# A mixture-of-experts kernel on one core: hand-set semaphores and a looped TensorE program in place of a scheduled, unrolled one

## The chip, the core and the metric

The kernel runs on one core of a Trainium2 chip. A core has a matrix engine (TensorE, "PE" in the profile, with its weight loads listed apart as "PEld"), a vector engine (VectorE, DVE), a scalar engine (ScalarE, ACT), GpSimd (POOL) and SyncE (SP), and 16 transfer engines that move data between the large memory (HBM) and the on-chip memory (SBUF). TensorE writes its sums to PSUM, from where VectorE and ScalarE copy them out. Engines run on their own and wait for one another by semaphores.

The metric is the device time of one execution in microseconds (us), the median of several runs.

## The reference

Eight experts, each with its own 256 tokens: a matrix product, a ReLU, a second matrix product. Inputs and output are fp32.

```python
n_experts, capacity, hidden, expert_hidden = 8, 256, 512, 2048
# x [8, 256, 512], w1 [8, 512, 2048], w2 [8, 2048, 512]
h = np.matmul(x, w1)
h = np.maximum(h, 0)
return np.matmul(h, w2).astype(np.float32)
```

x is 4.19 MB, w1 and w2 are 33.55 MB each, the output is 4.19 MB.

## The kernel before

The weights are cast from fp32 to bf16 on their way into SBUF, by transfers that GpSimd issues. Expert weights are loaded in pairs; each of w1 and w2 has two buffers of two experts. Only the last pair is loaded one expert at a time, and w2 of expert 7 in two halves. In w1 each partition holds four rows of an expert (32 KB read in one piece), in w2 sixteen rows (32 KB too).

```python
w1_v = w1.rearrange("e (p ko) n -> p e (ko n)", ko=K1)      # K1 = 4, P = 128
w2_v = w2.rearrange("e (p j) n -> p e (j n)", p=P)          # j = 16
...
GROUPS = [(0, 1), (2, 3), (4, 5), (6, 7)]
W1_LOADS = [(g,) for g in GROUPS[:-1]] + [((6,),), ((7,),)]
W2_LOADS = [(g, 0, K2) for g in GROUPS[:-1]] + [((6,), 0, K2), ((7,), 0, 8), ((7,), 8, K2)]
...
def load_w1(es):
    ...
    nc.gpsimd.dma_start(w1t[g][:, i:i + len(es), :], w1_v[:, es[0]:es[-1] + 1, :])
```

x comes in two transfers (1 MB through SyncE, then cast by VectorE; the rest through GpSimd) and is transposed on TensorE, 64 blocks of 128x128. Layer 1 of an expert is 64 matmuls of 256 columns, with w1 as the stationary operand; ScalarE applies the ReLU while it moves two blocks of F (128x512) at a time from PSUM to hT. Layer 2 is 32 matmuls of 512 columns, with hT as the stationary operand.

```python
def layer1(e):
    ...
    for pr in range(K2 // 2):
        h_ps = psum_h.tile([P, 2, C], FP32, name="h_ps")
        for s in range(2):
            j = pr * 2 + s
            for ko in range(K1):
                nc.tensor.matmul(h_ps[:, s, :], w1_r[:, ko, :, j], xT[:, ko, :, e, :],
                                 start=(ko == 0), stop=(ko == K1 - 1))
        nc.scalar.activation(hT[:, pr * 2:pr * 2 + 2, :]..., h_ps[:]..., Relu)
    return hT

def layer2(e, hT):
    ...
    for k, m in order:
        nc.tensor.matmul(o_ps[m][:], hT[:, k, m * P:(m + 1) * P],
                         w2t[g][:, e - g[0], k * H:(k + 1) * H],
                         start=(k == 0), stop=(k == K2 - 1))
        if k == K2 - 1:
            ...   # VectorE (for the last expert also ScalarE) copies o_ps to out_sb or out_last
```

For the first three pairs both first layers run before both second layers. The output of experts 0 to 6 leaves in one transfer of 3.67 MB; ahead of it, and before the last half of w2, stands a store of 3 KB to the same place, which the large one has to wait for. The output of expert 7 leaves by itself, through SyncE.

```python
for e, hT in zip(g, hs):
    layer2(e, hT or layer1(e))
    if e == 5:
        issue(E, E)
        store_first()
        loads.append(tail)      # the last half of w2 of expert 7
        issue(E, E)
    if e == E - 2:
        store()
nc.sync.dma_start(out_v[:, E - 1, :], out_last[:].rearrange("p m h -> p (m h)"))
```

Everything is unrolled: each matmul is an instruction of its own in TensorE's program, and the framework places the semaphores.

Of the kernel before, what the change touches and what calls it, by code (L numbers as in the profile page):

```python
# [1 line left out]

# [5 lines left out]

FP32 = mybir.dt.float32  # L10
BF16 = mybir.dt.bfloat16


@with_exitstack
def kernel(
    ctx: ExitStack,
    tc: tile.TileContext,
    x: bass.AP,
    w1: bass.AP,
    w2: bass.AP,  # L20
    out: bass.AP,
):
    nc = tc.nc
    P = 128
    E, C, H = x.shape
    F = w1.shape[2]
    MC = C // P
    K1 = H // P
    K2 = F // P

    R = E * C // P

    x_v = x.rearrange("e (pp r) k -> (e pp) (r k)", r=R)
    w1_v = w1.rearrange("e (p ko) n -> p e (ko n)", ko=K1)
    w2_v = w2.rearrange("e (p j) n -> p e (j n)", p=P)
    out_v = out.rearrange("e (p mo) k -> p e (mo k)", mo=MC)

    GROUPS = [(0, 1), (2, 3), (4, 5), (6, 7)]
    W1_LOADS = [(g,) for g in GROUPS[:-1]] + [((6,),), ((7,),)]
    W2_LOADS = [(g, 0, K2) for g in GROUPS[:-1]] + [((6,), 0, K2), ((7,), 0, 8), ((7,), 8, K2)]
    NG = max(len(g) for g in GROUPS)
    GROUP = {e: g for g in GROUPS for e in g}

    const = ctx.enter_context(tc.tile_pool(name="const", bufs=1))
    w1_pool = ctx.enter_context(tc.tile_pool(name="w1_pool", bufs=4 // NG))  # L50
    w2_pool = ctx.enter_context(tc.tile_pool(name="w2_pool", bufs=4 // NG))
    hT_pool = ctx.enter_context(tc.tile_pool(name="hT_pool", bufs=2))
    psum_t = ctx.enter_context(tc.tile_pool(name="psum_t", bufs=2, space=bass.MemoryType.PSUM))
    psum_h = ctx.enter_context(tc.tile_pool(name="psum_h", bufs=3, space=bass.MemoryType.PSUM))
    psum_o = ctx.enter_context(tc.tile_pool(name="psum_o", bufs=3, space=bass.MemoryType.PSUM))

    identity = const.tile([P, P], BF16, name="identity")
    xT = const.tile([P, K1, MC, E, P], BF16, name="xT")
    out_sb = const.tile([P, E - 1, MC, H], FP32, name="out_sb")
    out_last = const.tile([P, MC, H], FP32, name="out_last")  # L60

    HEAD = 4
    x_head = const.tile([P, HEAD * H], FP32, name="x_head")
    x_sb = w2_pool.tile([P, NG, K2 * H], BF16, name="w2_sb")[:, 0, :]

    w1t, w2t = {}, {}

    def load_x():
        nc.gpsimd.dma_start(x_sb[:, HEAD * H:], x_v[:, HEAD * H:])  # L69

    def load_w1(es):
        g = GROUP[es[0]]
        if es[0] == g[0]:
            w1t[g] = w1_pool.tile([P, NG, K1 * F], BF16, name="w1_sb")
        i = es[0] - g[0]
        nc.gpsimd.dma_start(w1t[g][:, i:i + len(es), :], w1_v[:, es[0]:es[-1] + 1, :])  # L76

    def load_w2(es, a, b):
        g = GROUP[es[0]]
        if es[0] == g[0] and a == 0:  # L80
            w2t[g] = w2_pool.tile([P, NG, K2 * H], BF16, name="w2_sb")
        i = es[0] - g[0]
        nc.gpsimd.dma_start(  # L83
            w2t[g][:, i:i + len(es), a * H:b * H],
            w2_v[:, es[0]:es[-1] + 1, a * H:b * H],
        )

    def store_first():


        nc.gpsimd.dma_start(  # L91
            out_v[:16, 0:5:2, :16], out_sb[:16, 0:5:2, 0, :16]
        )

    def store():
        nc.gpsimd.dma_start(  # L96
            out_v[:, :E - 1, :], out_sb[:].rearrange("p e m h -> p e (m h)")
        )

    def transpose_x():  # L100


        x_r = x_sb.rearrange("p (r2 m q ko) -> p r2 m q ko", m=MC, q=P, ko=K1)
        for i, (ko, m) in enumerate((ko, m) for ko in range(K1) for m in range(MC)):
            ps = psum_t.tile([P, R // MC, P], BF16, name="xt_ps")
            for r2 in range(R // MC):
                nc.tensor.transpose(ps[:, r2, :], x_r[:, r2, m, :, ko], identity[:])  # L107
            src = ps[:].rearrange("k r2 ep -> k ep r2")
            dst = xT[:, ko, m].rearrange("k e (pp r2) -> k (e pp) r2", r2=R // MC)
            if i % 2:  # L110
                nc.scalar.copy(dst, src)  # L111
            else:
                nc.vector.tensor_copy(dst, src)  # L113

    def layer1(e):
        g = GROUP[e]
        w1_r = w1t[g][:, e - g[0], :].rearrange("p (ko q j) -> p ko q j", ko=K1, j=K2)
        hT = hT_pool.tile([P, K2, C], BF16, name="hT")
        for pr in range(K2 // 2):
            h_ps = psum_h.tile([P, 2, C], FP32, name="h_ps")  # L120
            for s in range(2):
                j = pr * 2 + s
                for ko in range(K1):
                    nc.tensor.matmul(  # L124
                        h_ps[:, s, :],
                        w1_r[:, ko, :, j],
                        xT[:, ko, :, e, :],
                        start=(ko == 0),
                        stop=(ko == K1 - 1),
                    )  # L130
            nc.scalar.activation(  # L131
                hT[:, pr * 2:pr * 2 + 2, :].rearrange("p a c -> p (a c)"),
                h_ps[:].rearrange("p a c -> p (a c)"),
                mybir.ActivationFunctionType.Relu,
            )
        return hT

    def layer2(e, hT):
        g = GROUP[e]
        last = e == E - 1  # L140
        o_ps = [psum_o.tile([P, H], FP32, name="o_ps") for _ in range(MC)]
        if last:
            order = [(k, m) for k in range(K2) for m in range(MC)]
        else:
            order = [(k, m) for m in range(MC) for k in range(K2)]
        for k, m in order:
            nc.tensor.matmul(  # L147
                o_ps[m][:],
                hT[:, k, m * P:(m + 1) * P],
                w2t[g][:, e - g[0], k * H:(k + 1) * H],  # L150
                start=(k == 0),
                stop=(k == K2 - 1),
            )
            if k == K2 - 1:
                if last and m == 1:
                    nc.scalar.copy(out_last[:, m, :], o_ps[m][:])  # L156
                elif last:
                    nc.vector.tensor_copy(out_last[:, m, :], o_ps[m][:])  # L158
                else:
                    nc.vector.tensor_copy(out_sb[:, e, m, :], o_ps[m][:])  # L160

    loads = []
    for i, g in enumerate(GROUPS):
        own = [(load_w1, l) for l in W1_LOADS if l[0][0] in g]
        own += [(load_w2, l) for l in W2_LOADS if l[0][0] in g]
        own.sort(key=lambda f: (f[1][0][0], f[0] is load_w2))
        loads += [(i, *f) for f in own]
    tail = loads.pop()  # L170

    def issue(ready1, ready2):

        while loads:
            i, f, l = loads[0]
            if i >= (ready1 if f is load_w1 else ready2):
                break
            loads.pop(0)
            f(*l)

    B = 4 // NG
    nc.sync.dma_start(x_head[:], x_v[:, :HEAD * H])
    nc.vector.tensor_copy(x_sb[:, :HEAD * H], x_head[:])  # L183
    with tc.manual_schedule(engines={mybir.EngineType.PE, mybir.EngineType.Pool}):
        load_x()
        make_identity(nc, identity)
        issue(B, B - 1)
        transpose_x()
        for i, g in enumerate(GROUPS):
            issue(i + B, i + B)  # L190
            whole = len(g) > 1 and (g,) in W1_LOADS
            if whole:
                hs = [layer1(e) for e in g]
                issue(i + 1 + B, i + B)
            else:
                hs = [None] * len(g)
            for e, hT in zip(g, hs):
                layer2(e, hT or layer1(e))
                if e == 5:
                    issue(E, E)  # L200
                    store_first()
                    loads.append(tail)
                    issue(E, E)
                if e == E - 2:
                    store()
    nc.sync.dma_start(out_v[:, E - 1, :], out_last[:].rearrange("p m h -> p (m h)"))

# [1 line left out]
_INS = ['x', 'w1', 'w2']  # L209
# [26 lines left out]
```

## Time and profile before

| what | value |
|---|---|
| time, median of 3 runs | 181.25 us (181.23 to 181.43) |
| span of the profiled execution | 179.7 us |
| layer 1 matmuls, mean of 512 | 285 ns |
| layer 2 matmuls, mean of 248 | 393 ns |
| ReLU evictions, mean of 64 | 597 ns |
| copies of o_ps by VectorE, mean of 14 | 692 ns |
| loads of a pair of experts (6), issue to landing, median | 62.1 us |
| loads of one expert (3), issue to landing, median | 51.5 us |

The span is the profiled execution from its first to its last instruction; the time of a run is a little longer than it. A matmul's duration is that of one record from start to end: matmuls overlap, so that 64 of layer 1 take 7.15 us together. "Issue to landing" counts the time that a transfer stands behind others in the queue. In the slices, a digit is the busy share in tenths of one fortieth of the span.

### The profile page before, as it was taken

The numbers are of one execution on the slowest core, as the hardware profiler recorded it, in microseconds if no ns is written. First come the engines' busy times: TensorE is split into PE (matmuls) and PEld (weight loads), VectorE is DVE, ScalarE is ACT, GpSimd is POOL, SyncE is SP. The second block draws the span as 40 slices with busy tenths as digits, with TensorE's granted clock in tenths as the row PEclk, the third lists the DMA queues.
The fourth block names the chain that finished last, engine by engine and source line by source line (L and its number), as shares of the span: only waits on it lengthen the run. The fifth ranks groups of instructions, "written<-read, shape, count | busy, mean of one in ns | idle before, by whom it ended". The sixth has DMA issues, their size and how long they took to land.

```text
span 179.7 us, 1827 instructions
## 1 busy us (share of the span) xinstructions
PE 127.1 (71%) x824; PEld 90.5 (50%) x832; DVE 16.5 (9%) x20; ACT 44.1 (25%) x70; POOL 9.9 (6%) x20
## 2 busy tenths in 40 slices
PE   0017600899629991999569943999199999999960
PEld 0017500699514440899434412999034479469520
DVE  0205500000001111000002210000002210110010
ACT  2004400266500000266500000566100026116210
POOL 7000100000100001000100030000002000002000
PEclk9999975699978999699999997899969999999998
DMA  6999998999999899999999999999999999999995
GB/s 201 252 219 204 233 230 186 226 233 208 201 233 230 190 222 233 208 201 233 230 193 219 233 208 201 233 230 193 219 233 204 204 233 228 195 210 214 349 420 217
DMA packets 3735, 40.48 MB, mean 225 GB/s; under 512 B 272, under 2 KB 272, under 8 KB 1296
## 3 DMA queue, kind: packets, MB, share of 16 engines
q0 software_dynamic: 3440, 38.80, 96.8%
q1 hardware_dynamic: 288, 1.57, 2.4%
q8 instruction: 6, 0.10, 0.2%
q14 instruction: 1, 0.01, 0.0%
HBM read 71.30 MB, written 4.20 MB: 420 GB/s over the span
## 4 chain that ended last, share of the span: by engine, by line
PE 58%; DMA 27%; another core or an unknown queue 9%; POOL 1%; issue 1%; ACT 0%; POOLq 0%
PE o_ps L147 32%; DMA w_sb<-in_w_dram 27%; PE h_ps L124 25%; POOL w_sb L76 0%; POOL w_sb L69 0%; ACT out_last L156 0%; POOL identity masks.py:199 0%; POOL identity masks.py:197 0%; POOLq masks.py:199 0%; POOLq L220 0%
## 5 line engine op out<-in xcount | busy, mean ns | idle before, releaser
L124 PE MATMUL h_ps<-xT,w_sb 128*128 128x256 bf16 x512 | 61.3, 285 | 20.2 <-DMA w_sb<-in_w_dram 20.2
L124 PEld LDWEIGHTS <-w_sb 128*128 128x128 bf16 x512 | 58.3, 146 | 24.1 <-DMA w_sb<-in_w_dram 21.9
L147 PE MATMUL o_ps<-w_sb,hT 128*128 128x512 bf16 x248 | 58.6, 393 | 12.8 <-DMA w_sb<-in_w_dram 12.2
L131 ACT ACTIVATE hT<-h_ps 128x512 bf16<-128x512 f32 x64 | 38.2, 597 | 106.8 <-PE h_ps L124 106.8
L147 PEld LDWEIGHTS <-hT 128*128 128x128 bf16 x256 | 25.6, 101 | 44.3 <-issue 9.3
L160 DVE COPY out_sb<-o_ps 128x512 f32<-128x512 f32 x14 | 9.7, 692 | 128.7 <-PE o_ps L147 128.7
L107 PE MATMUL xt_ps<-identity,w_sb 128*128 128x128 bf16 x64 | 7.7, 309 | 13.8 <-DVE w_sb L183 6.9
L107 PEld LDWEIGHTS <-w_sb 128*128 128x128 bf16 x64 | 6.7, 145 | 14.6 <-DVE w_sb L183 6.9
L111 ACT COPY xT<-xt_ps 128x1024 bf16<-128x1024 bf16 x4 | 4.0, 1012 | 16.5 <-PE xt_ps L107 16.5
L83 POOL DMA_DIRECT2D w_sb<-in_w_dram x6 | 3.8, 637 | 53.6 <-PE o_ps L147 36.5
L113 DVE COPY xT<-xt_ps 128x1024 bf16<-128x1024 bf16 x4 | 4.9, 1224 | 10.2 <-PE xt_ps L107 10.2
L76 POOL DMA_DIRECT2D w_sb<-in_w_dram x5 | 3.3, 658 | 44.6 <-PE h_ps L124 44.6
L96 POOL DMA_DIRECT2D out_dram<-out_sb x1 | 1.0, 968 | 27.3 <-issue 27.3
L91 POOL DMA_DIRECT2D out_dram<-out_sb x1 | 0.6, 554 | 29.2 <-DVE out_sb L160 29.2
L156 ACT COPY out_last<-o_ps 128x512 f32<-128x512 f32 x1 | 0.6, 585 | 6.3 <-PE o_ps L147 6.3
L158 DVE COPY out_last<-o_ps 128x512 f32<-128x512 f32 x1 | 0.7, 692 | 13.4 <-PE o_ps L147 13.4
L183 DVE CAST w_sb<-x_head 128x2048 bf16<-128x2048 f32 x1 | 1.2, 1228 | 5.6 <-DMA x_head<-in_x_dram 5.6
L111 ACT ACT_TABLE_LOAD x1 | 1.3, 1283 | 0.7 <-PEq L220 0.7
L69 POOL DMA_DIRECT2D w_sb<-in_x_dram x1 | 0.7, 679 | 0.8 <-POOLq L220 0.8
masks.py:199 POOL TENSOR_SCALAR_AFFINE_SELECT identity<-identity 128x128 bf16<-128x128 bf16 x1 | 0.3, 287 | 0.1
masks.py:197 POOL MEMSET identity<- 128x128 bf16 x1 | 0.2, 223 | 0.0
L220 POOL MEMSET const-float32-0.0<- 128x1 f32 x1 | 0.1, 93 | 0.2 <-issue 0.2
(3 smaller groups left out, 0.3 us busy)
## 6 DMA issues: line engine op xcount, KB each, us to landing
w_sb<-in_w_dram POOLq DMA_DIRECT2D x6, 4096.0 KB, 62.1
w_sb<-in_w_dram POOLq DMA_DIRECT2D x3, 2048.0 KB, 51.5
out_dram<-out_sb POOLq DMA_DIRECT2D x1, 3584.0 KB, 12.9
w_sb<-in_w_dram POOLq DMA_DIRECT2D x2, 1024.0 KB, 44.7
w_sb<-in_x_dram POOLq DMA_DIRECT2D x1, 1536.0 KB, 11.6
x_head<-in_x_dram SPq DMA_DIRECT2D x1, 1024.0 KB, 4.8
out_dram<-out_last SPq DMA_DIRECT2D x1, 512.0 KB, 4.3
out_dram<-out_sb POOLq DMA_DIRECT2D x1, 3.0 KB, 27.8
```

The lines of the kernel that those rows point to most:

```text
L69: nc.gpsimd.dma_start(x_sb[:, HEAD * H:], x_v[:, HEAD * H:])
L76: nc.gpsimd.dma_start(w1t[g][:, i:i + len(es), :], w1_v[:, es[0]:es[-1] + 1, :])
L83: nc.gpsimd.dma_start(w2t[g][:, i:i + len(es), a * H:b * H], w2_v[:, es[0]:es[-1] + 1, a * H:b * H],)
L96: nc.gpsimd.dma_start(out_v[:, :E - 1, :], out_sb[:].rearrange("p e m h -> p e (m h)"))
L107: nc.tensor.transpose(ps[:, r2, :], x_r[:, r2, m, :, ko], identity[:])
L111: nc.scalar.copy(dst, src)
L113: nc.vector.tensor_copy(dst, src)
L124: nc.tensor.matmul(h_ps[:, s, :], w1_r[:, ko, :, j], xT[:, ko, :, e, :], start=(ko == 0), stop=(ko == K1 - 1),)
L131: nc.scalar.activation(hT[:, pr * 2:pr * 2 + 2, :].rearrange("p a c -> p (a c)"), h_ps[:].rearrange("p a c -> p (a c)"), mybir.ActivationF ...
L147: nc.tensor.matmul(o_ps[m][:], hT[:, k, m * P:(m + 1) * P], w2t[g][:, e - g[0], k * H:(k + 1) * H], start=(k == 0), stop=(k == K2 - 1),)
L160: nc.vector.tensor_copy(out_sb[:, e, m, :], o_ps[m][:])
L183: nc.vector.tensor_copy(x_sb[:, :HEAD * H], x_head[:])
```

## The change

The framework's scheduling is put aside: the whole program stands in one section whose semaphores are set by hand. TensorE's program becomes three loops (over the four blocks of x to be transposed; over the experts; inside that over the two halves of F), in which the operands in SBUF are addressed by bytes in registers, so that one body serves every expert. The registers of the next few matmuls are worked out in batches while the present ones run. The purpose is a short TensorE program and full control of who waits for what.

As one body serves all experts, all are laid out alike: four slots for w1 and four for w2, one expert each, loaded per expert and freed per expert; w2 is laid out in two halves, and F is gone through in two halves of 32 matmuls. The last expert's w1 and w2 are loaded by halves. SyncE waits for each load and then counts up one semaphore per weight matrix, from which TensorE takes one for each half. ScalarE evicts four blocks of F (128x1024) at a time. Second layers go through k with both halves of the tokens in turn, for all experts.

```diff
-    w2_v = w2.rearrange("e (p j) n -> p e (j n)", p=P)
+    w2_v = w2.rearrange("e (h p j) n -> p e h (j n)", h=2, j=JH)
...
-    GROUPS = [(0, 1), (2, 3), (4, 5), (6, 7)]
-    W1_LOADS = [(g,) for g in GROUPS[:-1]] + [((6,),), ((7,),)]
-    W2_LOADS = [(g, 0, K2) for g in GROUPS[:-1]] + [((6,), 0, K2), ((7,), 0, 8), ((7,), 8, K2)]
...
+    loads = []
+    for e in range(E - 1):
+        loads += [(1, e, 0, 2), (2, e, 0, 2)]
+    loads += [(w, E - 1, h, 1) for w in (1, 2) for h in range(2)]
+    d_w = [sem(f"d_w{i}") for i in range(len(loads))]
+
+    with tc.tile_critical(no_gpsimd_drain=True):
...
+        sp.dma_start(x_head[:], x_v[:, :HEAD * H]).then_inc(d_head, 16)
+        for i, (w, e, h, n) in enumerate(loads):
+            sp.wait_ge(d_w[i], 16)
+            sp.sem_inc(c_w1 if w == 1 else c_w2, n)
...
+            old = e - NS
+            if (w, e) == (2, 2):
+                pool.wait_ge(p_xt, K1 * MC)
+            if old >= 0 and h == 0:
+                if w == 1:
+                    pool.wait_ge(p_h, NG * (old + 1))
+                else:
+                    pool.wait_ge(p_o, MC * (old + 1))
...
+            elif n == 2:
+                src, dst = w1_v[:, e, :], w1_sb[:, e % NS, :]
             else:
+                cols = slice(h * FH, (h + n) * FH)
+                src = w1_v[:, e, :].rearrange("p (ko f) -> p ko f", ko=K1)[:, :, cols]
+                dst = w1_sb[:, e % NS, :].rearrange("p (ko f) -> p ko f", ko=K1)[:, :, cols]
+            pool.dma_start(dst, src).then_inc(d_w[i], 16)
...
+            for g in range(NG):
+                act.wait_ge(p_h, e * NG + g + 1)
+                act.activation(
+                    hT[:, g * GJ:(g + 1) * GJ, :].rearrange("p a c -> p (a c)"),
+                    h_ps[g % UG][:],
+                    mybir.ActivationFunctionType.Relu,
+                ).then_inc(c_h)
...
+        def take(s, n):
+            pe.wait_ge(s, n).then_inc(s, -n)
...
+        def compute(address, ids, regs):
+            for i, r in zip(ids, regs, strict=True):
+                base, offset = address(i)
+                pe.reg_add(r, base, offset)
...
+        CHUNKS1 = [(0, 5, lo[:5]), (5, 11, hi), (11, 17, lo), (17, 23, hi), (23, 29, lo), (29, 32, hi[:3])]
+        CHUNKS2 = [(0, 3, hi[3:]), (3, 9, lo), (9, 15, hi), (15, 16, lo[5:])]
...
+        def half():
+            take(c_w1, 1)
+            n = JH * K1
+            for i in range(n):
...
+                mm = matmul(
+                    h_ps[g][:, (j % GJ) * C:(j % GJ + 1) * C],
+                    at(w1_sb, r, [[JH, P]]),
+                    at(xT, reg[f"xt{ko}"], [[E * P, MC], [1, P]]),
+                    start_tensor_calc=ko == 0,
+                    stop_tensor_calc=ko == K1 - 1,
+                )
...
+        def expert():
+            loop("half", reg["half"], 2, half)
+            for k in range(K2):
+                if k % JH == 0:
+                    take(c_w2, 1)
...
+                for m in range(MC):
+                    mm = matmul(
+                        o_ps[m][:],
+                        pe.lower_ap(hT[:, k, m * P:(m + 1) * P], for_matmul_weights=True),
+                        at(w2_sb, r, [[1, H]]),
+                        start_tensor_calc=k == 0,
+                        stop_tensor_calc=k == K2 - 1,
+                    )
...
+        loop("expert", count, E, expert)
```

## The prediction

> **What bounds the kernel now.** I read the page first: engine busy times, slices, queues. Then the chain that ended last, in order of time. Then the timeline of the last 20 us and, for single loads, issue time plus time to landing.
>
> The page (engine, busy us, share, instructions; then the slices of DMA use; then the queues):
>
> ```profile
> span 179.7 us, 1827 instructions
> PE 127.1 (71%) x824; PEld 90.5 (50%) x832; DVE 16.5 (9%) x20; ACT 44.1 (25%) x70; POOL 9.9 (6%) x20
> ...
> DMA  6999998999999899999999999999999999999995
> ...
> q0 software_dynamic: 3440, 38.80, 96.8%
> q1 hardware_dynamic: 288, 1.57, 2.4%
> q8 instruction: 6, 0.10, 0.2%
> ...
> HBM read 71.30 MB, written 4.20 MB: 420 GB/s over the span
> ```
>
> The transfers are busy from the second slice to the last but one; no engine comes near that. 71.30 + 4.20 = 75.5 MB must move, whatever TensorE does. (The slices count bf16 bytes for casting loads, so I use the bytes on the fp32 side.)
>
> The chain of work that ended last (start us, duration us, what):
>
> ```profile
> 3.19 49.38 DMA w_sb<-in_w_dram
> ...
> 68.01 3.90 another core or an unknown queue
> 71.91 0.05 issue
> 71.96 15.87 PE h_ps L124 x128
> 87.82 3.44 another core or an unknown queue
> 91.27 0.05 issue
> 91.31 0.39 PE o_ps L147
> ...
> 105.30 5.32 another core or an unknown queue
> 110.62 0.05 issue
> 110.66 15.56 PE h_ps L124 x128
> 126.22 3.76 another core or an unknown queue
> ```
>
> Each stretch of matmuls ends, and TensorE then stands 3.4 to 5.3 us until the next weights land. The chain names TensorE for 58%, but that is work lying inside a transfer's time. The groups of waits call the "unknown queue" by its name: waits for w_sb<-in_w_dram. The landings that start stretches are 32.20 (from the timeline), 52.62, 71.96, 91.31, 110.66, 130.03. Differences: 20.42, 19.34, 19.35, 19.35, 19.37. A pair of experts' w1 is 2 x 512 x 2048 x 4 B = 8.39 MB; 8.39 MB / 19.35 us = 433 GB/s, the same in four of five steps. The first step is 1.07 us longer; I come back to it.
>
> The end, from the timeline:
>
> ```profile
> 164.73 0.97 POOL L96 DMA_DIRECT2D out_dram<-out_sb  x1 [27.26 <-issue]
> ...
> 173.90 0.58 ACT L156 COPY out_last<-o_ps 128x512 f32<-128x512 f32 x1 [6.31 <-PE o_ps L147]
> 174.51 0.35 SPq L206 DMA_DIRECT2D out_dram<-out_last  x1
> ```
>
> Issue plus time to landing: last half of w2 of expert 7 136.9 + 32.0 = 168.9; out_sb 164.7 + 12.9 = 177.6; out_last 174.5 + 4.3 = 178.8. Between 168.9 and 178.8 all 4.19 MB of output move, 424 GB/s: no pause either. So the end is a sum of transfers: 75.5 MB / 433 GB/s = 174.4 us, some 2 us until the first bytes move, and 2 to 3 us of small losses, up to 178.8; then 0.9 us until the span ends at 179.7, and 1.5 us that the time (181.25) has over the span.
>
> [...]
>
> **The change part by part.**
>
> *Instruction blocks removed.* q8's 0.2% of 16 engines' span is 0.002 x 16 x 179.7 = 5.8 us, over 6 packets 0.96 us each (coarse: the share is rounded). [...] So the first block should delay all later landings by about 1 us. The first pair step is 1.07 us long and none after it is[...]. I choose to read that 1.07 us as instruction fetch. The changed TensorE program has 16 + 32 + 32 = 80 matmuls with 80 weight loads, one register instruction per batch of additions (the built order shows one row each, some 20), a dozen waits and three branches: about 210[...]. If the loops stay held, no block is fetched while weights move: **-1.0 us**.
>
> *Shorter rows.* w2 is read by halves: rows of 16 KB in place of 32 KB for seven experts (expert 7 was halved before). Per engine (128 partitions / 16) that is 8 more rows an expert, 56 in all. w1 of expert 7 is loaded by column halves: rows of 4 KB, 64 per engine in place of 8, 56 more. The cost of a row from the end of the trace: 4.19 MB of output in 4 KB rows took 9.9 us where 433 GB/s gives 9.7, so 0.2 us for 64 rows an engine, 3.5 ns each. 112 x 3.5 ns = **+0.4 us**.
>
> *More loads.* 18 weight loads in place of 11. GpSimd spends 0.54 to 0.75 us issuing one, far ahead of need (times to landing 30 to 69 us), so issue is hidden. On the transfer engines a single expert takes 9.7 us against 19.35 / 2: at most 0.02 each. **+0.1 us**.
>
> *Entry and exit of the hand-set section.* The built order shows one more wait of all engines on SyncE before the first transfer and another after the last. The barrier in front of the first transfer now ends at about 0.7 us with others like it costing a few tenths. The exit now is 0.9 us with its own barriers. I put **+0.15 us** and **+0.2 us**, an estimate by likeness.
>
> *TensorE.* Per expert it now needs 7.15 us (64 matmuls with h_ps) and 7.07 us (32 with o_ps), 14.2 us; loads give it 19.35 us an expert, so 5.1 us of slack. [...] Starts with w1 of one expert in place of two and waits in other places stay inside the slack. ScalarE evicts 128x1024 in place of 128x512: 32 in place of 64, each under twice 0.6 us: hidden.
>
> *The tail.* Expert 7's first layer started at 159.75 when all its w1 was there, and ran 7.21 us; then 7.07 us of layer 2 to 173.9. With w1 in halves, half of that layer runs before 159.7. After the last half of w2 lands (168.9) 16 matmuls are left, 3.5 us: 172.5 in place of 173.9. That is worth nothing: out_last only joins the 3.67 MB of out_sb behind which the transfer engines are busy to the end.
>
> Sum: -1.0 + 0.4 + 0.1 + 0.15 + 0.2 = -0.15 us, so 181.1; the terms for entry and exit are the softest and may be nil, so I say **181.0 us**.
>
> **Rivals.** (1) *TensorE becomes the bound*: addresses from registers, or loop-backs that fetch blocks again, stretch an expert from 14.2 past 19.35 us, by a factor of 1.36. For it: every weight load and most moving operands now take an address from a register, and nothing in the trace shows what that costs[...]. Against it: the additions come in batches, ahead of use[...]. At 21 us an expert, eight experts behind a start at 22 us end at 190, and the time is about 195. (2) *The tail's gain counts*: if the outputs were not bound by bytes, 1.4 us would come off, 179.7. Against it: 424 GB/s from 168.9 to 178.8. (3) *A load waits for its slot*: slots free per expert, not per pair; w1 of expert 4 can be issued when expert 0's first layer is done, near 31 us, while the queue holds x and eight loads, 37.7 MB, up to about 90 us. Nothing to lose or gain: the loads of before never ran dry either. (4) *Row cost is larger when casting from HBM*: at 10 ns a row, +1.1 us in place of 0.4, and 181.8.
>
> **Range and chances.** The known terms are each below 1.1 us and of both signs; most of the range is whether the instruction blocks really cost 1 us, and rows and barriers: 180.0 to 182.2. Faster by over 2% would be under 177.6, which is less than the bytes need with the 1.5 us outside the span: 0.01. Slower by over 2% (above 184.9) needs rival 1: 0.06. The rest, 0.93, within 2%.
>
> **What would show it.** Right: no packets on the instruction queue, or one; TensorE still waiting several us for weights at each layer; single loads landing about 9.7 us apart, 19.4 us an expert; the last weights near 168.5; 424 GB/s after it. Row cost: w2 landings more than 9.72 us after w1 would mean I set it too low. Wrong: a chain with TensorE busy from expert to expert, matmul groups with "issue" as what ended the idle time, many packets on the instruction queue, or a slice of low transfer use before the last.

## The result, and the profile after

The changed kernel takes **187.89 us** (187.74 to 188.07, 6 runs) where the kernel before takes 181.33 (181.20 to 181.82, 6 runs): a ratio of **1.0358** (95% interval 1.0344 to 1.0372), 6.6 us more. The prediction was 181.0, with a range of 180.0 to 182.2.

The page of the changed kernel, the same parts as of the one before (busy times, slices of transfer use, what they moved, queues):

```profile
span 185.8 us, 2152 instructions
PE 130.4 (70%) x824; PEld 91.5 (49%) x832; DVE 15.9 (9%) x21; ACT 38.7 (21%) x38; POOL 14.2 (8%) x26
...
DMA  5969989999999999999999999999999999999990
GB/s 199 238 127 169 226 187 212 222 226 201 219 233 201 215 217 236 220 192 212 220 229 226 192 219 210 226 212 212 240 212 198 219 202 212 220 220 234 420 410 12
...
q0 software_dynamic: 5344, 38.80, 95.5%
q1 hardware_dynamic: 288, 1.57, 2.3%
q8 instruction: 1, 0.02, 0.0%
HBM read 71.30 MB, written 4.20 MB: 406 GB/s over the span
```

The same bytes move, and in the middle nothing is new: transfers are busy throughout. Two places differ. The third slice (9.3 to 13.9 us) has a 6, with 127 GB/s; and the last slice has a 0, where before it had a 5. Something holds the transfers up once near the start, and the span goes on for some us after the last of them. The instruction queue moved one block in place of six, a block being one packet on it (0.10 MB in 6 before, 0.02 MB in 1 now).

TensorE's timeline of the changed kernel (start us, duration us, group, and what ended the idle time before it), the first three experts:

```profile
26.11 9.07 PE L238 MATMUL h_ps<-xT,w_sb 128*128 x64 [2.91 <-PEq L213]
35.82 7.07 PE L238 MATMUL o_ps<-w_sb,hT 128*128 x31 [0.65 <-PEq L213]
45.55 8.85 PE L238 MATMUL h_ps<-xT,w_sb 128*128 x64 [2.66 <-PEq L213]
55.23 7.07 PE L238 MATMUL o_ps<-w_sb,hT 128*128 x31 [0.83 <-PEq L213]
65.98 8.85 PE L238 MATMUL h_ps<-xT,w_sb 128*128 x64 [3.68 <-PEq L213]
75.71 7.07 PE L238 MATMUL o_ps<-w_sb,hT 128*128 x31 [0.89 <-PEq L213]
```

L213 is TensorE's own semaphore wait, which here stands for a weight load: SyncE passes each landing on. TensorE idles before every layer, and layers start 9.7 us apart, the pace of the loads (before: 19.35 us a pair). So TensorE with its loops and registers is not the bound. But the first layer starts at 26.1 us, and one step, 55.23 to 65.98, is 10.75 us, about 1.05 more than the rest. The packet of the one instruction block starts inside this step, at 61.97 us, and takes 0.94.

GpSimd's timeline of the changed kernel, from its first transfer on:

```profile
1.46 0.69 POOL L121 DMA_DIRECT2D w_sb<-in_x_dram  x1 [1.01 <-DVE identity L169]
2.24 0.31 POOL masks.py:199 TENSOR_SCALAR_AFFINE_SELECT identity<-identity 128x128 bf16<-128x128 bf16 x1
13.45 3.11 POOL L152 DMA_DIRECT2D w_sb<-in_w_dram  x5 [10.90 <-issue]
```

and of the kernel before:

```profile
2.45 0.75 POOL L76 DMA_DIRECT2D w_sb<-in_w_dram  x1
```

Before, the first weight load was issued at 2.45 us. Now it is issued at 13.45, after 10.9 us in which GpSimd waits for nothing that a semaphore shows. The instructions of line 124 (least, median and most ns, start us) say what it did; the windows of the changed kernel (busy us by engine, granted clock, transfer share, GB/s) say what that left:

```profile
L124 POOLq DRAIN  x1: 11319/11319/11319, 1.6 to 1.6; - x1
```

```profile
12.80:14.70 1.90, 1.27 (x13) 1.28 (x14) 0.20 (x1) 0.00 (x0) 1.25 (x2) 1.00 0.00 0
```

Line 124 is a line of the change that the diff shown above does not have: `pool.drain().then_inc(s_ident)`, behind the identity. The drain lasts from 1.6 to 12.9 us; x, issued just before it, lands at 1.46 + 11.4 = 12.9. When it ends, everything that was queued has landed, and from 12.8 to 14.7 us no transfer runs at all.

At the other end, the instructions of the exit, of the changed kernel:

```profile
L431 POOLq DRAIN  x3: 46/131/1700, 183.1 to 185.5; - x3
...
L431 POOLq EVENT_SEMAPHORE_RANGE_CLEAR  x1: 268/268/268, 185.2 to 185.2; - x1
```

and of the kernel before:

```profile
L231 POOLq DRAIN  x3: 40/95/13525, 164.7 to 179.4; - x3
...
L231 POOLq EVENT_SEMAPHORE_RANGE_CLEAR  x1: 114/114/114, 179.3 to 179.3; - x1
```

The kernel before began its long drain at 164.7 us, under the stores, and it was over at 178.2 us: behind the landing of GpSimd's own store (177.6), ahead of the last landing (178.8), which was that of SyncE's store. In the changed kernel GpSimd's drain begins at 183.1, when all has landed (177.41 + 5.4 = 182.8), and still takes 1.70 us. From the last landing to the end of the span it is 3.0 us, before 0.9.

### The profile page after: what moved, and what is told of

It reads as the page before. It is cut to its first block, busy times and chain, and to the rows that moved or that the text cites. A ratio compares the mean times of both kernels' runs of the same rounds, so it can differ in the third digit from the quotient of the medians.

```text
span 185.8 us, 2152 instructions
## 1 busy us (share of the span) xinstructions
PE 130.4 (70%) x824; PEld 91.5 (49%) x832; DVE 15.9 (9%) x21; ACT 38.7 (21%) x38; POOL 14.2 (8%) x26
## 3 DMA queue, kind: packets, MB, share of 16 engines
q0 software_dynamic: 5344, 38.80, 95.5%
## 5 line engine op out<-in xcount | busy, mean ns | idle before, releaser
L238 PE MATMUL h_ps<-xT,w_sb 128*128 x512 | 66.7, 296 | 20.0 <-PEq L213 19.7
L238 PEld LDWEIGHTS h_ps<-xT,w_sb 128*128 x512 | 60.6, 148 | 27.9 <-issue 23.9
L238 PE MATMUL o_ps<-w_sb,hT 128*128 x248 | 56.3, 379 | 10.7 <-PEq L213 10.3
L199 ACT ACTIVATE hT<-h_ps 128x1024 bf16<-128x1024 f32 x32 | 32.8, 1024 | 111.7 <-PE h_ps L238 111.7
L238 PEld LDWEIGHTS o_ps<-w_sb,hT 128*128 128x128 bf16 x256 | 24.4, 98 | 40.5 <-issue 12.4
L152 POOL DMA_DIRECT2D w_sb<-in_w_dram x18 | 11.5, 645 | 89.5 <-PE h_ps L238 42.0
L238 PEld LDWEIGHTS xt_ps<-identity,w_sb 128*128 x64 | 6.5, 146 | 16.4 <-issue 16.4
L205 ACT COPY out_sb<-o_ps 128x512 f32<-128x512 f32 x1 | 0.6, 587 | 8.1 <-PE o_ps L238 8.1
## 6 DMA issues: line engine op xcount, KB each, us to landing
out_dram<-out_sb POOLq DMA_DIRECT2D x1, 3584.0 KB, 12.8
w_sb<-in_x_dram POOLq DMA_DIRECT2D x1, 1536.0 KB, 11.4
```

The costliest lines, as they stand in the source:

```text
L152: pool.dma_start(dst, src).then_inc(d_w[i], 16)
L199: act.activation(hT[:, g * GJ:(g + 1) * GJ, :].rearrange("p a c -> p (a c)"), h_ps[g % UG][:], mybir.ActivationFunctionType.Relu,).then_in ...
L205: act.copy(out_sb[:, E - 1, 1, :], o_ps[1][:]).then_inc(v_last)
L238: return pe.add_instruction(inst)
```

## The experiments

Each is the changed kernel with one edit, unless it says otherwise; times are medians, with the ratio to the kernel before on the same chip. Three suspects: GpSimd's first drain, the exit, and the shorter rows; and the question what instruction blocks cost.

**The first drain taken away.** TensorE learns of the identity from the instruction that makes it.

```diff
-        make_identity(nc, identity[:], nomemset=True)
-        pool.drain().then_inc(s_ident)
+        pool.affine_select(out=identity[:], in_=identity[:], ...).then_inc(s_ident)
```

> The identity's own instruction counts up the semaphore for TensorE; GpSimd's drain behind it is gone. Theory A (GpSimd's drain holds back the issue of the weights until the x transfer has landed, and the queue runs dry): the first weight load is issued near 2.5 us in place of 13.45, w1 of expert 0 lands near 22.5 us in place of 25.9, and the time falls by 3.4 us from 187.9 to 184.5. Rival B (loads per expert, or the layout of w2, start slower, whatever GpSimd does): issue moves but w1 of expert 0 still lands after 25 us, and the time stays at 187.9.

Measured: 184.32 us, ratio 1.0162 (1.0148 to 1.0176): 3.57 us less than the changed kernel. GpSimd's timeline in this run:

```profile
2.24 0.30 POOL L123 TENSOR_SCALAR_AFFINE_SELECT identity<-identity 128x128 bf16<-128x128 bf16 x1
2.48 3.11 POOL L159 DMA_DIRECT2D w_sb<-in_w_dram  x5
```

The first load lands at 2.48 + 20.2 = 22.7 us in place of 26.0 (13.45 + 12.5). From 12 to 15 us the transfer share is 1.13 here and 0.44 in the changed kernel (a packet is counted whole where it starts, so that a share can pass 1). Theory A holds, rival B falls: the loads per expert keep their pace once they are issued in time.

**The same drain put into the kernel before**, as the only edit.

```diff
         make_identity(nc, identity)
+        nc.gpsimd.drain()
         issue(B, B - 1)
```

> The kernel before with one line more: a GpSimd drain behind the identity, ahead of the weight loads. Theory A (the drain waits for the x transfer and the queue runs dry): first weight load issued near 13.4 us, first pair of w1 lands near 35.6 in place of 32.2, time 181.4 + 3.4 = 184.8. Rival (only the hand-set program suffers, as its identity waits for VectorE): 181.4.

Measured: 184.76 us, ratio 1.0197 (1.0183 to 1.0211), 3.45 us more. GpSimd's timeline of this run has the first weight load here, behind this drain:

```profile
13.25 0.75 POOL L76 DMA_DIRECT2D w_sb<-in_w_dram  x1 [10.74 <-issue]
...
L187 POOLq DRAIN  x1: 10562/10562/10562, 2.2 to 2.2; - x1
```

One line makes half of the loss in a kernel that has nothing else of the change. It is the drain, not the hand-set program around it.

**The drain kept, but x issued behind it.** Does a drain cost that much by itself, or does it wait for what is out?

```diff
-        pool.dma_start(x_sb[:, HEAD * H:], x_v[:, HEAD * H:]).then_inc(d_x, 16)
         pool.wait_ge(s_zero, 1)
         make_identity(nc, identity[:], nomemset=True)
         pool.drain().then_inc(s_ident)
+        pool.dma_start(x_sb[:, HEAD * H:], x_v[:, HEAD * H:]).then_inc(d_x, 16)
```

> The changed kernel with its first drain kept, but x issued behind it: GpSimd makes the identity, drains with no transfer outstanding, then issues x and the weights. Theory A (the drain waits for the transfers that are out, and costs little itself): the drain takes about 0.2 us in place of 11.3, x starts some 0.5 us later than now, the weights follow without a gap; time 187.9 - 3.57 + 0.5 = 184.8. The exit's drain takes about 1.78 us, as in the run without the first drain, if it is some 0.08 us for each transfer issued since the last drain (1.70 for 20, 1.62 for 19, 1.78 for 21). Rival (a drain on GpSimd is slow in itself at this place, or what is lost is the first use of the queue after it): 187.9 or above.

Measured: 185.18 us, ratio 1.0195 (1.0177 to 1.0213). The instructions of the drain's line in this run:

```profile
L123 POOLq DRAIN  x1: 379/379/379, 1.3 to 1.3; - x1
```

0.38 us in place of 11.32, the same instruction behind the identity. What it waited for was the transfer that GpSimd had issued; SyncE's part of x (issued at 0.95 us and landing 4.7 us later in the changed kernel) was still under way and did not hold it. The time is 0.4 us above what was expected. x was issued at 2.32 us, 0.86 later than in the changed kernel, where I had put 0.5; but x also took 12.5 us to land in place of 11.4, and no step of layers is about a microsecond too long in this run, so that the near agreement is in part chance. The drain at the exit took 1.778 us here, as expected.

**A drain behind the last store**, where GpSimd has nothing else to do.

```diff
             out_v[:, :E - 1, :], out_sb[:, :E - 1]...
         ).then_inc(d_out, 16)
+        pool.drain()
```

> GpSimd drains right after issuing the store of experts 0 to 6, while the stores still run, in place of only at the exit. Theory A (the exit is long because GpSimd's last drain, 1.70 us, starts only after the last landing and has its own work to do, which the kernel before had under the stores): the drain at the exit shrinks to about 0.1 us, the span's end comes 1.4 us after the last landing in place of 3.0, time 187.9 - 1.6 = 186.3. Rival B (a drain at the exit of the program costs 1.7 us wherever an earlier one stands): no change, 187.9. Rival C (barriers of the hand-set section, not the drain): no change either, and the time between barriers is as long as now.

Measured: 186.37 us, ratio 1.0265 (1.0251 to 1.0279): 1.52 us less. The instructions of the exit in this run:

```profile
L432 POOLq DRAIN  x3: 40/53/131, 183.0 to 184.0; - x3
```

Theory A holds: behind an earlier drain under the stores, the exit's longest takes 0.13 us in place of 1.70. The added drain lasts 13.73 us from 168.6 on and is over at 182.3, ahead of the last landing (177.30 + 5.4 = 182.7). Without it, the time goes by the count of transfers. The exit's drain takes 1.618 us where 19 transfers were issued on GpSimd since the last drain (the run with long rows), 1.700 where 20 (the changed kernel), 1.778 where 21 (the run without the first drain, and the one with x behind it): 0.08 us for each. Of the 2.1 us more at the exit, 0.6 remain, which no run took apart: one more barrier, and a clear of semaphores of 0.27 us in place of 0.11.

**Long rows again.** w2 with a partition's sixteen rows together, w1 of the last expert in one load.

```diff
-    w2_v = w2.rearrange("e (h p j) n -> p e h (j n)", h=2, j=JH)
+    w2_v = w2.rearrange("e (p h j) n -> p e h (j n)", h=2, j=JH)
-    loads += [(w, E - 1, h, 1) for w in (1, 2) for h in range(2)]
+    loads += [(1, E - 1, 0, 2)] + [(2, E - 1, h, 1) for h in range(2)]
     # and the columns of w1 in steps of K2, halves JH apart
```

> w2 in rows of 32 KB again (a partition holds sixteen rows of an expert, in two halves) and w1 of expert 7 in one load, all else as in the changed kernel. The theory (rows cost about 3.5 to 5 ns each per engine): single w2 loads land 9.68 us apart in place of 9.73, w1 of expert 7 takes 9.7 us in place of 9.88, the last weights land 0.5 us earlier, time 187.4. Rival (shorter rows cost nothing; the spacing of the landings is chance): 187.9. Rival (the later start of expert 7's first layer, when all its w1 is there, delays the end): 187.9 or above.

Measured: 187.20 us, ratio 1.0319 (1.0305 to 1.0333): 0.69 us less, of which 0.08 is the shorter drain at the exit (one load fewer).

**Short rows in the kernel before**, with its pairs and all else kept.

```diff
-    w2_v = w2.rearrange("e (p j) n -> p e (j n)", p=P)
+    w2_v = w2.rearrange("e (h p j) n -> p e h (j n)", h=2, j=K2 // 2)
     # w1 of expert 7 in two loads of half the columns; layer 1 indexes the columns likewise
```

> The kernel before with the rows of the changed one: w2 in rows of 16 KB, w1 of expert 7 in two column halves with rows of 4 KB, pairs as before. The theory (rows cost about 3.5 to 6 ns each per engine): 181.4 + 0.6 = 182.0. Rival (it was the loads of single experts, or the order, that cost 0.7 us): 181.4.

Measured: 181.92 us, ratio 1.0031 (1.0019 to 1.0042): 0.61 us more. Both ways round the rows cost about 0.6 us. Over 112 more rows an engine, the prediction's count, that is 5.4 ns a row, an estimate (the pages have 5344 packets on the queue in place of 3440, 119 more for each of 16 engines). The interval of this ratio, 0.34 to 0.76 us, leaves room for 3 to 7 ns. Each of the two edits also changes the number of loads by one, which was not taken apart from the rows.

**The loop over halves written out**, meant to bring blocks back with a longer loop body.

```diff
-            loop("half", reg["half"], 2, half)
+            half()
+            half()
```

> The inner loop over halves of F is written out twice[...]. Theory A (an instruction block costs a transfer engine 1.07 us[...], so that one block costs as much as six): more than one packet on the instruction queue, perhaps one or two per expert, and a time within 0.5 us of 187.9[...]. Rival B (each block costs about 1 us at the end): eight blocks more would be 8 us more, 196. Rival C (loop-backs stall TensorE until a block is fetched): TensorE idles at each expert's start with weights there; time above 189 only if that passes 5 us an expert.

Measured: 187.84 us, ratio 1.0348 (1.0334 to 1.0363), the same as the changed kernel. It told less than I wanted: the instruction queue moved one block here too. The edit did not do what it was meant to. Counted in the trace, a turn of this loop is 223 instructions (96 matmuls, 96 weight loads, 31 others); how many must stand in a loop before more blocks are fetched, this run does not show. No TensorE stall came of it (its longest wait before a first layer is 3.5 us, in the changed kernel 3.7), but rival C and the cost of blocks were hardly tested.

**All loops over experts written out too**, which makes the blocks come back.

```diff
-        loop("expert", count, E, expert)
+        for _ in range(E):
+            expert()
     # and the halves written out as above
```

> The changed kernel with its loops over experts and halves written out: the same instructions in the same order, without branches, some 1,900 on TensorE[...]. Theory A (the first block costs 1.07 us[...]): 6 or 7 packets on the instruction queue, time 187.9 to 188.4. Rival B (each block costs about 1 us at the end, as the prediction had it for the lot and as a sum would have it): 193 or more. If branches themselves had cost time on the path: below 187.9.

Measured: 188.50 us, ratio 1.0387 (1.0371 to 1.0403). Its queues:

```profile
q8 instruction: 7, 0.11, 0.2%
```

Seven blocks in place of one, and 0.6 us, not 6. That is a little over theory A's range and far below rival B's 193. Nor is the 0.6 us the price of six blocks. The first layer and the last half of the last one, in this run:

```profile
26.64 9.53 PE L238 MATMUL h_ps<-xT,w_sb 128*128 x64 [3.28 <-PEq L213]
...
173.71 3.62 PE L238 MATMUL o_ps<-w_sb,hT 128*128 x16 [0.59 <-PEq L213]
```

and the last half in the changed kernel, whose first layer starts at 26.11:

```profile
173.13 3.62 PE L238 MATMUL o_ps<-w_sb,hT 128*128 x16 [1.42 <-PEq L213]
```

The unrolled run is 0.53 us late at its first layer already, before its first block is fetched (41.1 us); what made it late stays open (0.14 of it is a later issue, 13.59 in place of 13.45). From there to the last half it takes 147.07 us with seven blocks, the changed kernel 147.02 with one. Six more blocks cost nothing that shows. What one costs is less even than the 1.05 us of the changed kernel suggests: of the seven other runs with a single block, six have a step that is 0.65 to 0.86 us too long, and one (with x behind the drain) has none. A run with no block at all was not made: even the looped program fetched one, and what called for it stays open.

**All three edits together.**

> The first drain gone, an earlier drain at the end, long rows: the three edits of the first experiments together. If the three losses are separate, they add: 187.89 - 3.57 - 1.52 - 0.69 = 182.1, with the last landing near 178.4 and 0.7 us above the kernel before, which would be the entry and exit of the hand-set section. Rival (they overlap, e.g. a later end hides a drain): 183 or above. Rival (TensorE becomes the bound once the weights come earlier): 183 or above, with TensorE no longer waiting for weights.

Measured: 182.71 us, ratio 1.0068 (1.0054 to 1.0082): 5.2 us of the 6.6 are back, 0.6 less than the sum. The chain that ended last in this run shows a new wait (start us, duration us, what):

```profile
159.19 0.04 issue
159.23 5.35 PE h_ps L246 x32
...
168.30 6.97 PE o_ps L246 x32
175.27 0.02 issue
175.29 0.58 ACT out_sb L213
```

With w1 of the last expert in one piece, its first layer starts only at 159.2 us, and its first half takes 5.35 us where the second takes 3.69. TensorE ends at 175.3, and the last output is issued at 175.91, later than the 174.5 us of the kernel before. That might be what is missing. So I ran the two drains alone, with the halves kept.

> The first drain gone and a drain behind the last store, short rows and the last expert's w1 in halves kept. If the terms add: 187.89 - 3.57 - 1.52 = 182.8. In the run of all three edits TensorE's tail became late (its last matmul at 175.3, for the last expert's w1 came in one piece), which may have eaten what the long rows gained; then this run comes out equal to that one, 182.7, although its rows are shorter, and its out_last is issued before 174.5 us. If it is above 183, the terms overlap.

Measured: 183.10 us, ratio 1.0087 (1.0073 to 1.0101); the last output is issued at 173.82 us. That is 0.3 us above the sum, so the terms overlap a little. Against all three edits the short rows cost 0.4 us here, not 0.69. The late tail is not shown to be the reason: the last output lands at 173.82 + 5.4 = 179.2 us here and at 175.91 + 3.3 = 179.2 there, although it was issued 2.1 us later. Where the missing 0.3 to 0.6 us went stays open. No version ran below the kernel before.

## Why the prediction was wrong

**What bounds the kernel: right.** The transfers bound it before and after. TensorE waits for weights before each layer, loads come 9.7 us apart, and the 4.19 MB of output follow without a pause. Rival 1 (TensorE becomes the bound) fell: 64 and 32 matmuls with register addresses and branches take 7.4 to 9.1 and 7.1 us (a branch 0.20 us in the median of 28), and idle time is left in front of every layer up to the last expert's first. Rival 2 (the tail counts) fell too.

**The step that failed first: "GpSimd spends 0.54 to 0.75 us issuing one, far ahead of need ..., so issue is hidden"**, and with it rival 3's "the loads of before never ran dry either". The sum had no term at all for `pool.drain()`, which stands between x and the first weight load. It waited for just that x, 11.32 us, and the queue ran dry, with no transfer from 12.8 to 14.7 us. Taking it away gave 3.57 us, putting it into the kernel before cost 3.45: more than half of the miss.

**The second: "I put +0.15 us and +0.2 us, an estimate by likeness".** The entry cost next to nothing on the path: x lands within 0.1 us of where it landed before (12.8). The exit was put at 0.2 and measured 2.1: 1.5 of it is the drain (1.70 us after the last landing), which the kernel before had under its stores, and for which likeness to its barriers was no guide.

**The third: "If the loops stay held, no block is fetched while weights move"**, for which 1.0 us was taken off. One block was fetched, and the prediction itself would have taken "no packets on the instruction queue, or one" as right. The reading behind it fits: one pair step was 1.07 us too long in the kernel before with its six blocks, and no later pair step was. But then going from six to one takes nothing off: the changed kernel has one such step too, of 1.05 us, and seven blocks took no more time than one. The gain was nil. That of six blocks only the first should count was my estimate; why one load was late and later ones were not, no run shows.

**Rows: the sign was right, and the size is not told apart from the prediction's.** It put 0.4 us; 0.69 and 0.61 were measured, and the interval of the second (0.34 to 0.76) holds 0.4. In the profiled runs the stretch between the first and the last weights is 0.4 longer.

**The sum again.** The landings of the profiled runs give it piece by piece (us from the span's start):

| | before | changed | more |
|---|---|---|---|
| x landed | 12.80 | 12.83 | 0.0 |
| first 8.39 MB of weights landed | 32.15 | 35.65 | 3.5 (first drain) |
| last weights landed | 168.91 | 172.78 | 0.4 (rows, loads and blocks together) |
| last output landed | 178.85 | 182.77 | 0.1 |
| end of the span | 179.7 | 185.8 | 2.1 (exit) |
| time of that run | 181.48 | 187.90 | 0.3 (outside the span) |

That is 6.4 us, all of what lies between these two runs. The 0.4 in the middle agrees with the blocks' gain being nil: the kernel before with short rows, which still has its six blocks, takes 137.1 us between the same two landings (32.20 to 169.34), the changed kernel 137.1, the kernel before 136.8.

## What to carry to other kernels

Where the queue of transfers is the bound, look at everything that the issuing engine does between two transfers, a drain of GpSimd above all: here it took 11.32 us behind a load of its own and 0.38 us ahead of it. Signalling from the instruction that makes the data gave 3.57 us. At the end of a kernel, a drain that ran under the last stores was over before the last landing here (182.3 and 182.7 us), and one that came after them took 1.62 to 1.78 us, 0.08 for each transfer issued. And a cost that was seen once need not grow with how often its cause occurs, nor shrink when some of the causes go: here one instruction block in a run went with a load that was late by up to 1.05 us, and seven cost no more than one.

## What the runs showed of the hardware that I had not expected

GpSimd's drain took 11.32 us with a load of its own in flight and 0.38 us with only SyncE's in flight. With everything landed it took 1.62, 1.70 and 1.78 us for 19, 20 and 21 transfers issued since the drain before, 0.08 us each, and 0.13 us when an earlier drain had been through. After the transfers had run dry, 1.3 us passed from the issue of the next load (13.4 us) until transfers were busy again (14.7 us). Each instruction block of the kernels before and after was one packet of 0.89 to 0.98 us. With a single block, one load was 0.65 to 1.05 us late in seven runs and none in the eighth; a run with seven blocks took as long from the first layer to the last as a run with one (147.07 and 147.02 us).
